# DeltaNet values: a convolution with tokens on the partitions, its shifted copies made by DMA

## The chip, the cores and the metric

The kernel runs on one core of a Trainium2 chip. The metric is the device time of one execution in microseconds (us). The engines are named as in the profile: PE (TensorE, matmuls and transposes), DVE (VectorE), ACT (ScalarE), POOL (GpSimd) and SP (SyncE, which here only issues transfers). Each engine runs its own instructions in the order in which they are written for it; engines wait for one another on semaphores.

## What is computed

Two layers of a hybrid decoder trunk for 256 tokens of width 2048. Each layer has one input projection whose columns feed a gated DeltaNet group (8 heads of 128) and an HGRN2 group; both outputs are concatenated, projected back and added, and a gated per-layer embedding is added after that. The part that matters here is the values of DeltaNet: a causal convolution over four tokens, one weight per channel and tap, then SiLU.

```python
def causal_conv(x, w):                    # x: tokens x channels, w: 4 taps x channels
    C = x.shape[-1]
    return lax.conv_general_dilated(
        x, w[:, None, :].astype(x.dtype), window_strides=(1,),
        padding=[(CONV_WIDTH - 1, 0)], dimension_numbers=("NWC", "WIO", "NWC"),
        feature_group_count=C)
...
qkv = jax.nn.silu(causal_conv(qkv.astype(f32), conv_w.astype(f32)))
q, k, v = jnp.split(qkv, 3, axis=-1)
```

So y[t] = w3·x[t] + w2·x[t−1] + w1·x[t−2] + w0·x[t−3], and v = y·sigmoid(y). The chunked delta rule then takes v scaled per token.

## The kernel before

**Weights and steps.** All large weight matrices are streamed in fp32 as 392 steps (`make_plan`, L79), most of them 128x1024 numbers, 512 KB. `load(n)` (L347) issues the transfer of a step's `raw` on SP's queue, `prep(n)` (L357) splits it: ACT rounds it to `whi` (L366), DVE subtracts to get the rest, `wlo` (L368). PE then takes three products per tile, activation-high by `whi`, activation-high by `wlo`, activation-low by `whi`, for both halves of the tokens (`products`, L380, recorded at L309): 12 matmuls for most steps. `ahead(n)` (L371) loads four steps ahead and splits two steps ahead; the pools hold three `raw` and three split pairs, so a raw buffer comes free when its `wlo` is done.

**Mixers.** The DeltaNet groups (`DN`, names `dn00` to `dn03` in layer 0 and `dn10` to `dn13` in layer 1, two heads each) and the HGRN2 groups (`HG`) are generators that are advanced once per weight step (`tick`, L331). At `yield self.wait("c")` a generator gives up PE's order for as many steps as the tables `DELAY` (L37) and `DELAY_AT` (L39) say for that point, and at `yield self.after("k")` until another part has been done. PE's instructions stay in that written order (`PEOrder`, L307); the order on DVE, ACT, POOL and SP comes from a scheduler, which weaves the mixers' work between the `wlo` and `whi` of the steps.

**The values.** `DN.dv` (L765) starts when the projection columns of `v` are complete: ACT evicts them, scaled per token, to `et` with the tokens on the partitions, 2 x 128 tokens by 256 channels (`evict`, L540, recorded at L544). A step later PE turns the four 128x128 blocks (`turned`, L547, tile `pvc`, recorded at L312), so that channels lie on the partitions and a shift by one token is a shift along the row. `conv` (L600) is then two scalings on ACT (L607) and six multiply-adds on DVE (L611); a sigmoid and a multiply (L770) give v. PE turns the four blocks back (tile `pv`), and DVE writes them, scaled by `invn` per token, to `R` (L777), which the delta rule reads. Queries and keys go through the same `conv`.

Of the kernel before, what the change touches and what calls it, by code (L numbers as in the profile page):

```python
# [8 lines left out]
F32 = mybir.dt.float32  # L9
F32R = mybir.dt.float32r  # L10
I32 = mybir.dt.int32
AF = mybir.ActivationFunctionType
ALU = mybir.AluOpType
PSUM = bass.MemoryType.PSUM

DEPTH, D, T, KT = 2, 2048, 256, 16
NG = 4
# [8 lines left out]
def chunk_cols(chunk):  # L26

    return [(START[k], 16) if k == "ba" else (START[k] + 256 * g, 256) for k, g in chunk]
# [8 lines left out]

DELAY_AT = {
# [115 lines left out]


@with_exitstack
def trunk(ctx: ExitStack, tc: tile.TileContext, head, xT, x, pT, W, par, fw, cst, msk, eye, out):
    nc = tc.nc
    pool = lambda name, bufs, **kw: ctx.enter_context(tc.tile_pool(name=name, bufs=bufs, **kw))
    cp = pool("const", 1)  # L160
# [8 lines left out]
    pm = pool("psm", 5, space=PSUM)  # L169

    V, S, G = nc.vector, nc.scalar, nc.gpsimd
# [16 lines left out]
    def xk(k, n=1):  # L188
        o = (0 if k // 4 else NNW) + T * (k % 4)
        return xt[k // 4][:, o:o + T * n]  # L190
# [54 lines left out]
    ident, ones, SL, UI = (cs[:, 128 * j:128 * j + 128] for j in range(4))  # L245
# [23 lines left out]
    def P(name, i, n=1):  # L269
        o = PAR[name][0] + i  # L270
        return pr[:, o:o + n]

    def bc(ap, n):
        return ap.unsqueeze(2).to_broadcast([ap.shape[0], ap.shape[1], n])

    def bc1(ap, n):
        return ap.unsqueeze(1).to_broadcast([ap.shape[0], n, ap.shape[1]])
# [36 lines left out]
    PE = PEOrder()  # L314
# [90 lines left out]
    def tmp(name, shape=(128, 512)):  # L405
        return tp.tile([128, 512], F32, tag="tmp", name=name)

    def sigmoid(dst, src, e=None):

        if e is None:  # L410
            S.activation(dst, src, AF.Exp, scale=-1.0)
            V.tensor_scalar(dst, dst, BIG, 1.0, ALU.min, ALU.add)
        else:
            S.activation(e, src, AF.Exp, scale=-1.0)
            V.tensor_scalar(e, e, BIG, None, ALU.min)
            V.tensor_scalar(dst, e, 1.0, None, ALU.add)
        S.activation(dst, dst, AF.Ln)
        S.activation(dst, dst, AF.Exp, scale=-1.0)
# [4 lines left out]
    def small(tag, n=4):  # L423
        return sp.tile([128, n], F32, tag=tag, name=tag)
# [36 lines left out]
    def first_squares(kp):  # L461

        sq = mp.tile([128, 512], F32, tag="R", name=f"x2{kp}", bufs=2) if not kp else tmp(f"x2{kp}")
        S.activation(sq, xk(2 * kp, 2), AF.Square)
# [46 lines left out]
    def mix(tag, n, bufs, name):  # L511
        return mp.tile([128, n], F32, tag=tag, name=name, bufs=bufs)

    def v4(ap):
        return ap.rearrange("p (a b) -> p a b", b=128)
# [24 lines left out]
    def evict(ps, c0, n, rt, name):  # L540

        et = mix("et", 1024, 2, name + "et")[:, :2 * n].rearrange("p (t n) -> p t n", t=2)
        for t in range(2):
            S.activation(et[:, t], ps[t][:, c0:c0 + n], AF.Copy, scale=rt[:, t:t + 1])  # L544
        return et

    def turned(et, c0, name):  # L547

        ps = pm.tile([128, 512], F32, tag="m", name=name)
        for i in range(4):  # L550
            hh, t = divmod(i, 2)
            PE.transpose(ps[:, 128 * i:128 * i + 128], et[:, t, c0 + 128 * hh:c0 + 128 * hh + 128], ident)
        return ps

    def rms_factor(f, ss):
        S.activation(f, ss, AF.Ln, scale=1.0 / 128, bias=epsc)
        S.activation(f, f, AF.Exp, scale=-0.5)

    class DN:
# [40 lines left out]
        def conv(self, ps, which):  # L600
# [12 lines left out]
            sigmoid(sg, ac)  # L613
            return ac, sg

        def conv_silu_kq(self, ps, which, w):
            ac, sg = self.conv(ps, which)
            for hh in range(2):
                V.tensor_tensor(self.kq[:, hh, :, w, :], v4(ac[:, 256 * hh:256 * hh + 256]),
                                v4(sg[:, 256 * hh:256 * hh + 256]), ALU.mult)  # L620
# [143 lines left out]

        def dv(self, ps, c0):  # L765
            n, kq, g = self.n, self.kq, self.g
            et = evict(ps, c0, 256, self.row.rt, n + "v")
            yield self.wait("c")
            ac, sg = self.conv(turned(et, 0, n + "pvc"), 2)
            V.tensor_tensor(ac, ac, sg, ALU.mult)  # L770
            yield self.wait("v")
            yield self.after("k")
            pv = pm.tile([128, 512], F32, tag="m", name=n + "pv")
            for i in range(4):
                PE.transpose(pv[:, 128 * i:128 * i + 128], ac[:, 128 * i:128 * i + 128], ident)
            R = v4(mix("R", 512, 2, n + "R"))
            V.tensor_tensor(R, v4(pv), bc(self.invn, 128), ALU.mult)  # L777
            yield self.after("T")
            yield self.wait("z0")
            v1 = v4(mix("v1", 512, 1, n + "v1"))  # L780

            pz = pm.tile([128, 512], F32, tag="m", name=n + "pz0")
            for hh in range(2):
                PE.matmul(pz[:, 128 * hh:128 * hh + 128], self.Tt[:, 2 * hh], R[:, 2 * hh], start=True, stop=True)
            V.tensor_tensor(v1[:, 0::2], v4(pz)[:, 0:2], bc(self.b[:, 0::2], 128), ALU.mult)
            yield self.wait("S")
            pS = pm.tile([128, 512], F32, tag="m", name=n + "pS")
            for hh in range(2):
                PE.matmul(pS[:, 128 * hh:128 * hh + 128], v4(self.ktail)[:, hh], v1[:, 2 * hh], start=True, stop=True)
            St = v4(mix("St", 256, 1, n + "St"))  # L790
            S.copy(St, v4(pS)[:, 0:2])
            yield self.wait("w")

            pw = pm.tile([128, 512], F32, tag="m", name=n + "pw")
            for hh in range(2):
                for w in range(2):
                    PE.matmul(pw[:, 256 * hh + 128 * w:256 * hh + 128 * w + 128], kq[:, hh, 1, w, :], St[:, hh],
                              start=True, stop=True)
            for hh in range(2):
                V.scalar_tensor_tensor(R[:, 2 * hh + 1], pw[:, 256 * hh:256 * hh + 128], self.neG[:, hh:hh + 1],  # L800
                                       R[:, 2 * hh + 1], ALU.mult, ALU.add)
            qs = v4(mix("qs", 256, 1, n + "qs"))
            V.tensor_tensor(qs, v4(pw)[:, 1::2], bc(self.eG, 128), ALU.mult)
            yield self.wait("z1")
            pz = pm.tile([128, 512], F32, tag="m", name=n + "pz1")
            for hh in range(2):
                PE.matmul(pz[:, 128 * hh:128 * hh + 128], self.Tt[:, 2 * hh + 1], R[:, 2 * hh + 1], start=True, stop=True)
            V.tensor_tensor(v1[:, 1::2], v4(pz)[:, 0:2], bc(self.b[:, 1::2], 128), ALU.mult)
            yield self.wait("o")
            po = pm.tile([128, 512], F32, tag="m", name=n + "po")  # L810
            for i in range(4):
                PE.matmul(po[:, 128 * i:128 * i + 128], self.QK[:, i], v1[:, i], start=True, stop=True)
            o = v4(tmp(n + "o"))
            S.copy(o[:, 0::2], v4(po)[:, 0::2])
            V.tensor_tensor(o[:, 1::2], v4(po)[:, 1::2], qs, ALU.add)
            ss = small("sso")
            for i in range(4):
                S.activation(sp.tile([128, 128], F32, tag="junk", name="junk", bufs=1), o[:, i], AF.Square,
                             scale=self.nq[:, i:i + 1], accum_out=ss[:, i:i + 1])
            f = small("fo")  # L820
            rms_factor(f, ss)
            V.tensor_tensor(f, f, self.nq, ALU.mult)
            yield self.wait("y")
            yield self.after("z")
            yield from head_norm(o, f, self.sz, P("dnw", self.l), g, self.y, n, self.wait("yp"))
# [299 lines left out]
    for l in range(DEPTH):  # L1125
# [7 lines left out]
        ps = {}  # L1133
# [16 lines left out]
        for c, k4 in order:  # L1150
# [5 lines left out]
            w = 2 if sum(n for _, n in chunk_cols(ch)) > 272 else 4  # L1156
# [26 lines left out]
        ps = {}  # L1183
# [20 lines left out]
        ps = {}  # L1204
        for c, k4 in order:
# [12 lines left out]
            if end and k4[3] == KT - 5:  # L1218

                n = state["next"]  # L1220
# [50 lines left out]
```

## Time and profile before

| what | us |
| --- | --- |
| median of 3 runs (lowest, highest) | 1284.66 (1283.68, 1284.71) |
| profiled execution | 1285.03 |
| its span, first to last instruction | 1283.3 |
| mean granted clock of PE | 0.997 |
| DMA engines, mean busy share in the tenths of the page | 4 to 8 tenths |

The profiled execution is 1.7 us longer than its span. In the page, `wlo<-raw,whi` names what an instruction writes and what it reads; `x394 | 482.9, 1227 | 257.6` are the count, the busy time in us, the mean of one in ns, and the time that the engine was idle just before such instructions. In a timeline the first number is the start, the second the duration, both in us. PE's matmuls overlap, so the distance of two starts says what one costs, not its duration.

### The profile page before, as it was taken

The page shows a single profiled execution, that of the slowest core. Times are in us where ns is not written, and L with a number is a line of the kernel's source. Part 1 is how long each engine was busy: PE and PEld are TensorE (multiplying, and loading weights), DVE is VectorE, ACT ScalarE, POOL GpSimd, SP SyncE. Part 2 cuts the span into 40 slices and gives each one's busy share as a digit, 9 for nine tenths or more (in the row PEclk, how much of TensorE's full clock was granted, in tenths as well). Part 3 has the DMA queues.
Part 4 walks back from the last instruction along what each step waited for, and adds up shares of the span by engine and source line. Part 5 has one row for each costly group of instructions (what it writes and reads, how often), then busy time and mean ns, then how long its engine had stood idle before and what let it go on. Part 6 is the DMA issues. An engine that isn't in the chain of part 4 may idle for free.

```text
span 1283.3 us, 19310 instructions
## 1 busy us (share of the span) xinstructions
PE 1262.2 (98%) x7112; PEld 1054.2 (82%) x7112; DVE 925.7 (72%) x1728; ACT 785.2 (61%) x1400; POOL 61.5 (5%) x55
## 2 busy tenths in 40 slices
PE   7999999999999999999999999999999999999996
PEld 6988888888888888888888888878888888888885
DVE  7789678787796855547568886897877958555475
ACT  7666766656665654437557667667656766544464
POOL 0100010010000000000001000100100000000010
PEclk9999999999999999999999999999999999999998
DMA  8565445445454455555555554544555545555563
GB/s 273 182 225 180 160 155 165 142 142 186 158 183 150 133 171 181 188 190 185 185 188 170 171 173 150 170 133 141 175 180 169 162 149 165 181 183 185 180 197 132
DMA packets 78751, 220.91 MB, mean 172 GB/s; under 512 B 15552, under 2 KB 25280, under 8 KB 78656
## 3 DMA queue, kind: packets, MB, share of 16 engines
q1 hardware_dynamic: 59840, 212.19, 50.9%
q10 hardware_dynamic: 18816, 7.48, 2.1%
q8 instruction: 56, 0.92, 0.3%
q14 instruction: 39, 0.32, 0.1%
HBM read 214.93 MB, written 4.72 MB: 171 GB/s over the span
## 4 chain that ended last, share of the span: by engine, by line
PE 91%; DVE 5%; ACT 1%; issue 1%; DMA 0%; SPq 0%; DVEq 0%; ACTq 0%
PE out L309 14%; PE gate L309 14%; PE in1hf L309 6%; PE in0hf L309 6%; PE in0dv L309 6%; PE in1dv L309 6%; PE in0dk L309 6%; PE in1dk L309 6%; PE in0hi L309 6%; PE in1hi L309 5%; PE up L309 2%; DVE wlo L368 1%; PE in0dz L309 1%; PE in1dz L309 1%; ACT whi L366 1%
## 5 line engine op out<-in xcount | busy, mean ns | idle before, releaser
L368 DVE TENSOR_TENSOR wlo<-raw,whi 128x1024 fp32r<-128x1024 f32 (+1 forms) x394 | 482.9, 1227 | 257.6 <-ACT whi L366 255.8
L366 ACT ACTIVATE whi<-raw 128x1024 fp32r<-128x1024 f32 (+1 forms) x394 | 413.4, 1051 | 360.7 <-PE out L309 88.3
L309 PE MATMUL in1hf<-whi,n1hi 128*128 128x512 f32 x128 | 52.5, 410 | 0.0
L309 PE MATMUL in1hi<-whi,n1hi 128*128 128x512 f32 x128 | 51.5, 402 | 0.0
L309 PE MATMUL in1dk<-whi,n1hi 128*128 128x512 f32 x128 | 51.1, 399 | 0.0
L309 PE MATMUL in1dk<-wlo,n1hi 128*128 128x512 f32 x128 | 50.1, 391 | 0.2 <-DVE wlo L368 0.2
L309 PE MATMUL gate<-whi,g0hi 128*128 128x512 f32 x128 | 50.1, 392 | 0.0
L309 PE MATMUL in1hf<-whi,n1lo 128*128 128x512 f32 x128 | 50.1, 391 | 0.0
L309 PE MATMUL in1hi<-whi,n1lo 128*128 128x512 f32 x128 | 50.0, 391 | 0.0
L309 PE MATMUL in1hf<-wlo,n1hi 128*128 128x512 f32 x128 | 50.0, 391 | 0.0
L309 PE MATMUL in1hi<-wlo,n1hi 128*128 128x512 f32 x128 | 50.0, 390 | 0.0
L309 PE MATMUL in1dk<-whi,n1lo 128*128 128x512 f32 x128 | 49.9, 390 | 0.0
L309 PE MATMUL gate<-whi,g1hi 128*128 128x512 f32 x128 | 49.9, 390 | 0.0
L309 PE MATMUL gate<-whi,g0lo 128*128 128x512 f32 x128 | 49.8, 389 | 0.0
L309 PE MATMUL gate<-wlo,g0hi 128*128 128x512 f32 x128 | 49.8, 389 | 0.0
L309 PE MATMUL gate<-whi,g1lo 128*128 128x512 f32 x128 | 49.8, 389 | 0.0
L309 PE MATMUL gate<-wlo,g1hi 128*128 128x512 f32 x128 | 49.8, 389 | 0.0
L309 PE MATMUL in1dv<-whi,n1hi 128*128 128x512 f32 (+1 forms) x128 | 48.3, 377 | 0.0
L309 PE MATMUL in1dv<-whi,n1lo 128*128 128x512 f32 (+1 forms) x128 | 46.6, 364 | 0.0
L309 PE MATMUL in1dv<-wlo,n1hi 128*128 128x512 f32 (+1 forms) x128 | 46.6, 364 | 0.0
L309 PE MATMUL in0hf<-whi,n0hi 128*128 128x512 f32 x96 | 39.2, 408 | 0.0
L309 PE MATMUL in0hi<-whi,n0hi 128*128 128x512 f32 x96 | 38.5, 401 | 0.0
(1549 smaller groups left out, 3251.2 us busy)
## 6 DMA issues: line engine op xcount, KB each, us to landing
raw<-W SPq DMA_DIRECT2D x384, 512.0 KB, 3.4
raw<-W SPq DMA_DIRECT2D x7, 544.0 KB, 4.5
h<-x SPq DMA_DIRECT2D x4, 512.0 KB, 5.4
xt<-xT SPq DMA_DIRECT2D x3, 512.0 KB, 7.0
out_dram<-h SPq DMA_DIRECT2D x6, 256.0 KB, 2.1
fw<-fw ACTq DMA_DIRECT2D x2, 512.0 KB, 5.4
pin<-pT ACTq DMA_DIRECT2D x2, 256.0 KB, 3.2
out_dram<-h ACTq DMA_DIRECT2D x2, 256.0 KB, 3.0
```

The costliest lines, as they stand in the source:

```text
L309: return tc.keep_in_program_order(nc.tensor.matmul(*a, **k))
L366: S.activation(hi[:, sl], raw[:, sl], AF.Copy)
L368: V.tensor_tensor(lo[:, sl], raw[:, sl], hi[:, sl].bitcast(F32), ALU.subtract)
```

## The change

`dv` no longer turns anything on PE. A new function `conv_tokens` leaves the tokens on the partitions: it makes three copies of `et`, shifted down by 1, 2 and 3 partitions, with transfers issued by SP. Each has a large transfer inside the columns of both token halves (L629: 127, 126 and 125 rows of 2 KB) and a small one for the rows that pass from the first half of the tokens to the second (L630); POOL zeroes the rows ahead of the first token (L628). The weights, which now vary along the row, come from a new input `cvw`, spread over 128 partitions on the host, 512 KB per group, loaded by SP (L621). DVE multiplies the unshifted tile by the last tap (L634), then each shifted tile by its tap (L636) and adds it (L637). The final scaling by `invn` and by the sigmoid goes straight to `R` in four instructions (L801). The wait "c" of the values is gone, and six distances of the mixers are other ones. `conv` stays for queries and keys. Line numbers of the changed code are those of the changed kernel.

```diff
 DELAY_AT = {
     "b1g": 5,
-    "d0D": 6, "d0k": 6, "d0p16": 4, "d0p32": 3, "d0p64": 1, "d0q": 7, "d0t64": 3, "d0v": 6,
-    "d1S": 3, "d1p64": 1, "d1q": 6, "d1ssq": 3, "d1t16": 4, "d1t32": 1, "d1yp": 2,
-    "d2D": 9, "d2k": 3, "d2t64": 4, "d2y": 4, "d2yp": 2, "d2z1": 2,
+    "d0k": 6, "d0p16": 4, "d0p32": 3, "d0p64": 1, "d0q": 7, "d0t64": 3, "d0v": 6,
+    "d1S": 2, "d1T": 8, "d1p64": 1, "d1q": 6, "d1ssq": 3, "d1t16": 4, "d1y": 4, "d1yp": 2,
+    "d2D": 9, "d2S": 2, "d2k": 3, "d2t64": 4, "d2y": 4, "d2yp": 2, "d2z1": 2,
...
+        def conv_tokens(self, ps, c0):
+            n, l, g = self.n, self.l, self.g
+            wv = mix("cvw", 1024, 1, n + "cvw")
+            nc.sync.dma_start(out=wv, in_=cvw[l * NG + g])
+            full = mix("et", 1024, 2, n + "vet")
+            et = full[:, :512]
+            for t in range(2):
+                S.activation(et[:, 256 * t:256 * t + 256], ps[t][:, c0:c0 + 256], AF.Copy, scale=self.row.rt[:, t:t + 1])
+            xs = [full[:, 512:1024], tmp(n + "vs2"), tmp(n + "vs3")]
+            for j, x in enumerate(xs, 1):
+                G.memset(x[0:j, 0:256], 0.0)
+                nc.sync.dma_start(out=x[j:128], in_=et[0:128 - j])
+                nc.sync.dma_start(out=x[0:j, 256:512], in_=et[128 - j:128, 0:256])
+            w = lambda j: bc1(wv[:, 256 * j:256 * j + 256], 2)
+            v2 = lambda ap: ap.rearrange("p (t n) -> p t n", t=2)
+            ac = tmp(n + "vac")
+            V.tensor_tensor(v2(ac), v2(et), w(3), ALU.mult)
+            for j, x in enumerate(xs, 1):
+                V.tensor_tensor(v2(x), v2(x), w(3 - j), ALU.mult)
+                V.tensor_tensor(ac, ac, x, ALU.add)
+            sg = tmp(n + "vsg")
+            sigmoid(sg, ac)
+            return ac, sg
...
         def dv(self, ps, c0):
             n, kq, g = self.n, self.kq, self.g
-            et = evict(ps, c0, 256, self.row.rt, n + "v")
-            yield self.wait("c")
-            ac, sg = self.conv(turned(et, 0, n + "pvc"), 2)
-            V.tensor_tensor(ac, ac, sg, ALU.mult)
+            ac, sg = self.conv_tokens(ps, c0)
             yield self.wait("v")
             yield self.after("k")
-            pv = pm.tile([128, 512], F32, tag="m", name=n + "pv")
-            for i in range(4):
-                PE.transpose(pv[:, 128 * i:128 * i + 128], ac[:, 128 * i:128 * i + 128], ident)
             R = v4(mix("R", 512, 2, n + "R"))
-            V.tensor_tensor(R, v4(pv), bc(self.invn, 128), ALU.mult)
+            for i in range(4):
+                hh, t = divmod(i, 2)
+                sl = slice(256 * t + 128 * hh, 256 * t + 128 * hh + 128)
+                V.scalar_tensor_tensor(R[:, i], ac[:, sl], self.invn[:, i:i + 1], sg[:, sl], ALU.mult, ALU.mult)
```

How this moves the order of instructions is shown at two places. The first is DVE around the values of group `dn11`, before (numbers behind names of `wlo` and `raw` are the step, those behind the underscore tell buffers apart):

```order
L368 TENSOR_TENSOR wlo238_7662<-raw238_7568,whi238_7661 128x1024
L412 TENSOR_SCALAR dn11sz_7651<-dn11sz_7651 128x512
L368 TENSOR_TENSOR wlo239_7712<-raw239_7627,whi239_7711 128x1024
L611 SCALAR_TENSOR_TENSOR dn11vac_7694<-dn11pvc_7689,pr_89,dn11vac_7694 128x255
L611 SCALAR_TENSOR_TENSOR dn11vac_7694<-dn11pvc_7689,pr_89,dn11vac_7694 128x254
L611 SCALAR_TENSOR_TENSOR dn11vac_7694<-dn11pvc_7689,pr_89,dn11vac_7694 128x253
L611 SCALAR_TENSOR_TENSOR dn11vac_7694<-dn11pvc_7689,pr_89,dn11vac_7694 128x255
L368 TENSOR_TENSOR wlo240_7748<-raw240_7659,whi240_7747 128x1024
```

The same place on DVE in the changed kernel, where `dn11vet` is both `et` and, in its second half, the copy shifted by one token:

```order
L634 TENSOR_TENSOR dn11vac_7681<-dn11vet_7667,dn11cvw_7665 128x512
L368 TENSOR_TENSOR wlo238_7708<-raw238_7588,whi238_7707 128x1024
L412 TENSOR_SCALAR dn11sz_7697<-dn11sz_7697 128x512
L636 TENSOR_TENSOR dn11vet_7667<-dn11vet_7667,dn11cvw_7665 128x512
L368 TENSOR_TENSOR wlo239_7738<-raw239_7647,whi239_7737 128x1024
L637 TENSOR_TENSOR dn11vac_7681<-dn11vac_7681,dn11vet_7667 128x512
L636 TENSOR_TENSOR dn11vs2_7670<-dn11vs2_7670,dn11cvw_7665 128x512
L636 TENSOR_TENSOR dn11vs3_7671<-dn11vs3_7671,dn11cvw_7665 128x512
L637 TENSOR_TENSOR dn11vac_7681<-dn11vac_7681,dn11vs2_7670 128x512
L368 TENSOR_TENSOR wlo240_7774<-raw240_7705,whi240_7773 128x1024
```

The first multiply of a shifted copy (L636) now stands ahead of the `wlo` of step 239, and four more rows ahead of that of step 240. On SP the transfers for this group stand between the weight loads of steps 240 and 241, in the changed kernel:

```order
L351 DMA raw240_7705<-W 128x1024
L630 DMA dn11vet_7667<-dn11vet_7667 1x16x16
L630 DMA dn11vs2_7670<-dn11vet_7667 2x256
L630 DMA dn11vs3_7671<-dn11vet_7667 3x256
L629 DMA dn11vet_7667<-dn11vet_7667 127x512
L629 DMA dn11vs2_7670<-dn11vet_7667 126x512
L629 DMA dn11vs3_7671<-dn11vet_7667 125x512
L351 DMA raw241_7735<-W 128x1024
```

Before, SP had only the weight loads there. The second place is DVE around the values of `dn12`, before:

```order
L368 TENSOR_TENSOR wlo271_8912<-raw271_8814,whi271_8911 128x1024
L815 TENSOR_TENSOR dn11o_8873<-dn11po_8868,dn11qs_8782 128x2x128
L701 TENSOR_TENSOR dn12pr1_8927<-dn12fx_8753 32x1
L704 TENSOR_REDUCE dn12fx_8753<-dn12pr1_8927 32x1
L701 TENSOR_TENSOR dn12pr2_8930<-dn12fx_8753 32x2x2
```

And in the changed kernel:

```order
L368 TENSOR_TENSOR wlo270_8924<-raw270_8790,whi270_8923 128x1024
L839 TENSOR_TENSOR dn11o_8865<-dn11po_8860,dn11qs_8768 128x2x128
L634 TENSOR_TENSOR dn12vac_8897<-dn12vet_8883,dn12cvw_8881 128x512
L636 TENSOR_TENSOR dn12vet_8883<-dn12vet_8883,dn12cvw_8881 128x512
L412 TENSOR_SCALAR dn12sz_8913<-dn12sz_8913 128x512
L637 TENSOR_TENSOR dn12vac_8897<-dn12vac_8897,dn12vet_8883 128x512
L636 TENSOR_TENSOR dn12vs2_8886<-dn12vs2_8886,dn12cvw_8881 128x512
L636 TENSOR_TENSOR dn12vs3_8887<-dn12vs3_8887,dn12cvw_8881 128x512
L637 TENSOR_TENSOR dn12vac_8897<-dn12vac_8897,dn12vs2_8886 128x512
L368 TENSOR_TENSOR wlo271_8942<-raw271_8842,whi271_8941 128x1024
```

The multiply of all three shifted copies and two of the additions have moved ahead of the `wlo` of step 271, which before stood ahead of all of the convolution.

More of the change, by code (lines that the diff above doesn't have):

```diff
@@ L156, in trunk @@
 @with_exitstack
-def trunk(ctx: ExitStack, tc: tile.TileContext, head, xT, x, pT, W, par, fw, cst, msk, eye, out):
+def trunk(ctx: ExitStack, tc: tile.TileContext, head, xT, x, pT, W, par, cvw, fw, cst, msk, eye, out):
     nc = tc.nc
@@ L766, in dv @@
             n, kq, g = self.n, self.kq, self.g
-            et = evict(ps, c0, 256, self.row.rt, n + "v")
-            yield self.wait("c")
-            ac, sg = self.conv(turned(et, 0, n + "pvc"), 2)
-            V.tensor_tensor(ac, ac, sg, ALU.mult)
+            ac, sg = self.conv_tokens(ps, c0)
             yield self.wait("v")
             yield self.after("k")
-            pv = pm.tile([128, 512], F32, tag="m", name=n + "pv")
+            R = v4(mix("R", 512, 2, n + "R"))
             for i in range(4):
-                PE.transpose(pv[:, 128 * i:128 * i + 128], ac[:, 128 * i:128 * i + 128], ident)
-            R = v4(mix("R", 512, 2, n + "R"))
-            V.tensor_tensor(R, v4(pv), bc(self.invn, 128), ALU.mult)
+                hh, t = divmod(i, 2)
+                sl = slice(256 * t + 128 * hh, 256 * t + 128 * hh + 128)
+                V.scalar_tensor_tensor(R[:, i], ac[:, sl], self.invn[:, i:i + 1], sg[:, sl], ALU.mult, ALU.mult)
             yield self.after("T")
@@ L1259 @@
         "par": np.ascontiguousarray(par),
+        "cvw": np.ascontiguousarray(np.broadcast_to(
+            a["dn_conv_w"][:, :, 2048:].reshape(DEPTH, 4, NG, 256).transpose(0, 2, 1, 3).reshape(DEPTH * NG, 1, 1024),
+            (DEPTH * NG, 128, 1024))),
         "fw": np.ascontiguousarray(np.broadcast_to(a["final_norm_w"], (128, D))), "cst": cst, "msk": msk,
```

## Prediction

> **What bounds the kernel now.** I read the page from its busy shares to its chain, then the waits of PE, then the costliest group of DVE.
>
> ```profile
> span 1283.3 us, 19310 instructions
> PE 1262.2 (98%) x7112; PEld 1054.2 (82%) x7112; DVE 925.7 (72%) x1728; ACT 785.2 (61%) x1400; POOL 61.5 (5%) x55
> PE 91%; DVE 5%; ACT 1%; issue 1%; DMA 0%; SPq 0%; DVEq 0%; ACTq 0%
> L368 DVE TENSOR_TENSOR wlo<-raw,whi 128x1024 fp32r<-128x1024 f32 (+1 forms) x394 | 482.9, 1227 | 257.6 <-ACT whi L366 255.8
> ```
>
> PE is busy for 98% of the span and makes 91% of the chain; the other engines only keep it fed. Its own waits, in the view of waits for PE alone, are these (total, times, longest):
>
> ```profile
> PE in0dz L309 <- ACT whi L238: 6.7, 3, 4.5
> PE dn02pv L312 <- DVE dn02vac L770: 0.7, 1, 0.7
> PE dn11pp L309 <- DVE dn11T L726: 0.7, 1, 0.7
> PE dn01pp L309 <- DVE dn01T L726: 0.7, 1, 0.7
> PE in1dk L309 <- DVE wlo L368: 0.2, 1, 0.2
> ```
>
> Apart from the start (6.7 us), PE waits for nothing worth naming: 0.2 us for `wlo`, the low half of the weights, in 392 steps. So whatever leaves PE is a gain at full price. And DVE makes every `wlo` in its own program order, 1.23 us each, with 257.6 us of idle time before them: DVE has room on average, but an instruction that stands before a `wlo` and waits for something late holds up that `wlo`, and after it PE.
>
> **What leaves PE.** Per head group 2 groups of 4 transposes, 16 groups in all. One of them in the timeline of PE, with the matmuls on both sides:
>
> ```profile
> 692.66 0.39 PE L309 MATMUL in1hf<-wlo,n1hi 128*128 128x512 f32 x1
> 692.89 0.39 PE L309 MATMUL in1hf<-whi,n1lo 128*128 128x512 f32 x1
> 693.12 0.60 PE L312 MATMUL dn10pvc<-cs,dn10vet 128*128 128x128 f32 x4
> 693.47 0.48 PE L309 MATMUL in1hf<-whi,n1hi 128*128 128x512 f32 x1
> 693.79 0.40 PE L309 MATMUL in1hf<-wlo,n1hi 128*128 128x512 f32 x1
> ```
>
> Big matmuls start 0.23 us apart. From 692.89 to 693.79 there are two of them and the group: 0.90 − 2 × 0.227 = 0.45 us. 16 × 0.45 = 7.1 us. The wait of `dn02pv`, 0.7 us, goes with it: 7.8 us gained, if nothing else becomes late.
>
> **What DVE and ACT do instead.** Rows for the durations, from the tile views and the timeline of DVE:
>
> ```profile
> L611 DVE SCALAR_TENSOR_TENSOR dn11vac<-dn11pvc,pr,dn11vac x6: 475/482/484, 777.9 to 781.3; 128x255 f32<-128x255 f32 x2, 128x254 f32<-128x254 f32 x2, 128x253 f32<-128x253 f32 x2
> 785.38 0.64 DVE L770 TENSOR_TENSOR dn11vac<-dn11vac,dn11vsg 128x512 f32<-128x512 f32 x1
> 790.57 0.69 DVE L777 TENSOR_TENSOR dn11R<-dn11pv,invn 128x512 f32<-128x512 f32 x1 [0.85 <-PE dn11pv L312]
> L800 DVE SCALAR_TENSOR_TENSOR dn11R<-dn11pw,neG,dn11R x2: 343/347/351, 882.9 to 883.1; 128x128 f32<-128x128 f32 x2
> 800.34 0.42 DVE L412 TENSOR_SCALAR hg10sz<-hg10sz 128x512 f32<-128x512 f32 x1
> 67.15 0.76 DVE L619 TENSOR_TENSOR dn00kq<-dn00qac,dn00qsg 128x256 f32<-128x256 f32 x2
> 61.82 0.47 DVE L611 SCALAR_TENSOR_TENSOR dn00qac<-dn00pqc,pr,dn00qac 128x253 f32<-128x253 f32 x1
> ```
>
> Per group DVE loses 6 × 0.48 + 0.64 + 0.69 = 4.2 us and gets 7 × 0.64 + 4 × 0.35 = 5.9 us: 1.7 us more, 8 times 13 us, beside 257.6 us of idle time; ACT loses the two scalings at L607. As throughput this is nothing. POOL's three memsets come long before their tiles are read (POOL is busy for 5%). The eight loads of `cvw` are 4 MB on a queue that moves 212 MB, and are issued a group ahead. The new distances move tiny PE groups by one step; the work that feeds them keeps its order, and the two 0.7 us waits for `pp` bound what they can give or take: I put 0, at most 1.4 either way.
>
> **The copies.** The disputed item is the copy of 127 rows of 2 KB by one row (L629), 254 KB: DVE's multiply of that tile (L636) waits for it, and stands right in front of a `wlo`. No transfer of before has a row count that 16 doesn't divide. The nearest rows:
>
> ```profile
> raw<-W SPq DMA_DIRECT2D x384, 512.0 KB, 3.4
> xt<-xT SPq DMA_DIRECT2D x3, 512.0 KB, 7.0
> dn11d<-dn11Bt ACTq DMA_DIRECT2D x1, 256.0 KB, 2.2
> q1 hardware_dynamic: 59840, 212.19, 50.9%
> ```
>
> The lower end is 2.2 us, the 256 KB of `dn11Bt`. For the upper end: 212.19 MB in 50.9% of 16 engines' 1283.3 us is 20.3 GB/s for one DMA engine; 254 KB on a single one are 12.8 us, and on 16 they are 0.8 us. So if all rows go to one engine the copy lands 2.2 − 0.8 + 12.8 = 14.2 us after its issue. 127 is prime, and the order of the changed kernel shows the same split at work: the copy of one row of 256 (L630) is issued as 16 pieces of 16, the one of 127 rows as it stands. [...]
>
> [...]
>
> What stands behind the waiting multiply, place by place: the evictions of `v` (first row: the last of the two starts at the second time, and takes 0.47 us) and the first matmul that reads the `wlo` in question.
>
> ```profile
> L544 ACT ACTIVATE dn00vet<-in0dv,s0rt x2: 473/478/482, 57.6 to 58.5; 128x256 f32<-128x256 f32 x2
> 64.71 0.39 PE L309 MATMUL in0hf<-wlo,n0hi 128*128 128x512 f32 x1
> L544 ACT ACTIVATE dn11vet<-in1dv,s1rt x2: 475/476/477, 770.1 to 771.4; 128x256 f32<-128x256 f32 x2
> 781.25 0.39 PE L309 MATMUL in1hi<-wlo,n1hi 128*128 128x512 f32 x1
> L544 ACT ACTIVATE dn12vet<-in1dv,s1rt x2: 456/462/469, 886.2 to 887.7; 128x256 f32<-128x256 f32 x2
> 897.35 0.39 PE L309 MATMUL in1hi<-wlo,n1hi 128*128 128x512 f32 x1
> L544 ACT ACTIVATE dn03vet<-in0dv,s0rt x2: 474/474/475, 332.6 to 334.0; 128x256 f32<-128x256 f32 x2
> 341.63 0.39 PE L309 MATMUL in0hf<-wlo,n0hi 128*128 128x512 f32 x1
> L544 ACT ACTIVATE dn10vet<-in1dv,s1rt x2: 455/465/475, 688.5 to 689.9; 128x256 f32<-128x256 f32 x2
> 704.21 0.39 PE L309 MATMUL in1hf<-wlo,n1hi 128*128 128x512 f32 x1
> ```
>
> - `dn00`, step 18: 59.0 + 13 + 0.64 (multiply) + 0.47 (a `qac` row) + 1.23 = 74.3, needed at 64.7: PE stalls 9.6 us.
> - `dn11`, step 239 (`dn01` has the same order): 771.9 + 13 + 0.64 + 1.23 = 786.8, needed at 781.25: 5.5 us, twice, 11 us.
> - `dn12`, step 271 (`dn02` likewise): behind the multiply stand `sz`, an addition, the second and third multiply and another addition: 888.2 + 13 + 0.64 + 0.42 + 4 × 0.64 + 1.23 = 906.0, needed at 897.35: 8.7 us; the third copy lands behind the first on its engine and may add 0.9. I take 9, twice, 18 us.
> - `dn03`, step 98 (`dn13` likewise): 334.5 + 13 + 0.64 + 1.23 = 349.4, needed at 341.6: 7.7 us; the next `wlo` has five more rows and the third copy ahead of it, which I estimate at 1.3. 9 us, twice, 18 us.
> - `dn10`, step 216: 690.4 + 13 + 0.64 + 0.76 + 4 × 0.64 + 1.23 = 708.6, needed at 704.2: 4.4 us.
>
> Together 61 us. The places lie some 80 us apart or more (58, 334 and 690, 771, 888 in the rows above), which at 257.6 idle in 1283 us leaves DVE some 16 us to catch up in, so nothing is carried over. The weight loads issued behind the copies sit on the same engine's queue, but each waits for a raw buffer that the late `wlo` itself frees, and lands some 3 to 5 us before PE, shifted by the stall, needs it: 0, with a rival for more.
>
> **Sum.** 1285.0 (this execution: its span and 1.7 us around it) − 7.8 + 61 = 1338.3; the median of the runs shown lies 0.4 below the profiled execution: 1338.
>
> **The rivals.**
> A (forecast): one engine carries the 127 rows. The sum moves by 8 us for each us of the landing: at 11 us 1322, at 15 us 1354. Likeliest range 1316 to 1360.
> B, the other side: the rows spread over the engines as every transfer of before does, and land after 2.2 us. DVE's order then has room at all eight places (in `dn12` 888.2 + 2.2 + 0.64 + 0.42 + 2.56 + 1.23 = 895.3, needed at 897.35), and only PE's relief is left: 1284.7 − 7.8, and some 1 us back at `dn00`, where DVE is fullest: 1278. For it: the largest transfers of before land within 7.0 us (`xt`, twice the size, at the crowded start). Against it: 127 can't be dealt out evenly, and the single row was cut on purpose. The mechanism decides at a landing of about 6 us: there `dn00` (2.6), `dn02` and `dn12` (2 each), `dn03` and `dn13` (0.7 each) eat the 7.8.
> C: one engine, and the loads queued behind the copies are late as well. Then it is as if the landing took 3 us more: 24 us on top, 1362. For it: SP issues both. Against it: the buffers, above.
> D: one engine that is about twice as fast, so that landing and gain cancel: 1285. Against it: the row of q1.
>
> **Chances.** A 0.79, C 0.06, B 0.13, D 0.02. Differences under 0.2% (2.6 us) can't be told from no change. Faster 0.13 (B), same 0.02 (D), slower 0.85 (A and C). The predicted time is A's. For the range I reach from a landing of 9 us (1306, lower still if a place hides more than I think: 1302) to C's 1366; B is left out whole, with what A and C have outside, not quite 2 in 10.
>
> **What would show it.** Right: the copies `vet<-vet` of 254 KB land about 13 us after their issue, those of 126 rows a little after them on the queue; PE's view of waits gets eight entries, `in..hf` and `in..hi` of layers 0 and 1 on DVE `wlo`, of 4 to 10 us each and about 60 us together; the idle time before DVE's L636 is about as large as the copies take; PE's busy time falls by some 7 us. Wrong: if the copies land in 2 to 3 us, the forecast falls whole and B holds; if they are late but PE waits for `raw` and `whi` instead of `wlo`, it is C; if they are late and PE doesn't wait, I have misread the order of DVE.

## The result

The changed kernel takes 1370.03 us (median of 4 runs, 1369.76 to 1372.78) against 1284.68 us: 1.0667 times as long, with a 95% interval of 1.0654 to 1.0680. The sign and the mechanism were as forecast, the size was not: 85 us were lost where 53 were forecast, and the time lies 4 us above the range.

The profile after, in the order of the prediction's views. First the page:

```profile
span 1368.0 us, 19330 instructions
PE 1272.7 (93%) x7048; PEld 1057.5 (77%) x7048; DVE 937.2 (69%) x1752; ACT 779.5 (57%) x1384; POOL 84.7 (6%) x79
PEclk9989999989989999999999999999898999999998
PE 82%; DMA 8%; DVE 6%; ACT 1%; issue 1%; SPq 1%; ACTq 0%; DVEq 0%
```

PE's share falls from 98% to 93%, and DMA, which had no part in the chain, has 8% of it. But PE is also busy for 10.5 us more than before with 64 instructions fewer, and the row of the granted clock has gaps that it did not have. Then the waits of PE (total, times, longest):

```profile
PE in0hf L309 <- DVE wlo L368: 21.3, 2, 12.0
PE in0hi L309 <- DVE wlo L368: 19.1, 2, 12.0
PE in1hi L309 <- DVE wlo L368: 18.7, 2, 11.6
PE in1hf L309 <- DVE wlo L368: 10.5, 3, 9.3
PE in0dz L309 <- ACT whi L238: 5.7, 3, 4.6
PE dn10pg L309 <- DVE dn10kq L645: 5.1, 1, 5.1
PE in0dk L309 <- DVE wlo L368: 1.3, 1, 1.3
PE in1dk L309 <- DVE wlo L368: 0.8, 1, 0.8
PE dn10px L309 <- ACT dn10P L761: 0.8, 1, 0.8
```

They add up to 83.3 us, where the five rows of before make 9.0: 74.3 us more. With the 10.5 us of busy time this is the whole difference of the spans, 1368.0 − 1283.3 = 84.7 us. And this is what `wlo` waited behind, in the waits of DVE:

```profile
DVE dn03vet L636 <- DMA dn03vet<-dn03vet: 12.7, 1, 12.7
DVE dn13vet L636 <- DMA dn13vet<-dn13vet: 12.7, 1, 12.7
DVE dn01vet L636 <- DMA dn01vet<-dn01vet: 11.5, 1, 11.5
DVE dn11vet L636 <- DMA dn11vet<-dn11vet: 11.4, 1, 11.4
DVE dn02vet L636 <- DMA dn02vet<-dn02vet: 10.8, 1, 10.8
DVE dn00vet L636 <- DMA dn00vet<-dn00vet: 10.5, 1, 10.5
DVE dn12vet L636 <- DMA dn12vet<-dn12vet: 10.5, 1, 10.5
DVE dn10vet L636 <- DMA dn10vet<-dn10vet: 10.3, 1, 10.3
```

Eight places, one for each group, each a wait of the first multiply for the copy of 127 rows. The rows of the tile `dn11vet` give the landing: SP issues that copy at 826.8, 0.6 us after the eviction, and the multiply starts at 840.4, 13.6 us later (at the eight places 13.6 to 15.0 us):

```profile
L629 SPq DMA_DIRECT2D dn11vet<-dn11vet x1: 631/631/631, 826.8 to 826.8; - x1
L636 DVE TENSOR_TENSOR dn11vet<-dn11vet,dn11cvw x1: 691/691/691, 840.4 to 840.4; 128x512 f32<-128x512 f32 x1
```

The one engine can be seen directly. Up to 831.0 SP is still issuing the next copy, so that only the 127 rows are under way, and the view of stretches of time (each row: the stretch, its length, busy time of PE, weight loads, DVE, ACT and POOL, then clock, DMA share and GB/s) gives

```profile
830.00:831.50 1.50, 1.50 (x9) 1.22 (x8) 0.00 (x0) 0.63 (x1) 0.77 (x1) 1.00 0.07 26
```

One of 16 engines is a share of 0.06, and at 26 GB/s the 254 KB take 10.0 us.

The busy time is in the timeline of PE, at the end of the stall of `dn00`:

```profile
75.84 0.79 PE L309 MATMUL in0hf<-wlo,n0hi 128*128 128x512 f32 x1 [12.04 <-DVE wlo L368]
76.43 0.63 PE L309 MATMUL in0hf<-whi,n0lo 128*128 128x512 f32 x1
76.86 0.63 PE L309 MATMUL in0hf<-whi,n0hi 128*128 128x512 f32 x1
...
81.47 0.39 PE L309 MATMUL in0hf<-wlo,n0hi 128*128 128x512 f32 x1
81.70 0.39 PE L309 MATMUL in0hf<-whi,n0lo 128*128 128x512 f32 x1
```

Behind the stall matmuls start 0.43 us apart, and only some 5 us later 0.23 us apart again. The stretches of time with the granted clock show why (the stall begins at 75.84 − 12.04 = 63.8):

```profile
63.80:67.00 3.20, 0.00 (x1) 0.00 (x0) 0.00 (x0) 0.87 (x1) 0.00 (x0) 1.00 0.32 103
67.40:75.80 8.40, 0.00 (x0) 0.00 (x0) 2.23 (x4) 0.63 (x1) 0.00 (x0) 0.50 0.14 45
75.80:80.60 4.80, 4.76 (x11) 3.69 (x12) 4.80 (x9) 1.26 (x2) 1.93 (x1) 0.50 0.66 199
81.20:83.00 1.80, 1.80 (x10) 1.49 (x9) 1.47 (x2) 1.47 (x8) 1.80 (x1) 1.00 0.61 228
```

PE idles, its clock is halved, and it works on at half speed before full speed is granted again: here the clock falls 3.2 to 3.6 us after PE went idle and is back at 1.00 some 5 us after work resumed. In steps of 0.2 us, the same view gives 2.0 to 4.8 us for the fall at the eight stalls, and 3.1 to 5.4 us for the return. A shorter stall can be enough, as one of 1.9 us below shows. The prediction's sum had no term for any of this.

### The profile page after: what moved, and what is told of

Same layout as the page of the kernel before. It is cut to its first block, busy times and chain, and to the rows that moved or that the text cites. A ratio compares the mean times of both kernels' runs of the same rounds, so it can differ in the third digit from the quotient of the medians.

```text
span 1368.0 us, 19330 instructions
## 1 busy us (share of the span) xinstructions
PE 1272.7 (93%) x7048; PEld 1057.5 (77%) x7048; DVE 937.2 (69%) x1752; ACT 779.5 (57%) x1384; POOL 84.7 (6%) x79
## 2 busy tenths in 40 slices
DMA packets 83422, 231.33 MB, mean 169 GB/s; under 512 B 16136, under 2 KB 25904, under 8 KB 83328
## 4 chain that ended last, share of the span: by engine, by line
PE 82%; DMA 8%; DVE 6%; ACT 1%; issue 1%; SPq 1%; ACTq 0%; DVEq 0%
PE out L309 13%; PE gate L309 13%; PE in0hi L309 6%; PE in1hi L309 6%; PE in0dv L309 6%; PE in1dv L309 6%; PE in0dk L309 5%; PE in1dk L309 5%; PE in0hf L309 5%; PE in1hf L309 4%; DVE wlo L368 2%; PE up L309 2%; DMA dn10vet<-dn10vet 1%; DMA dn00vet<-dn00vet 1%; PE in0dz L309 1%
## 5 line engine op out<-in xcount | busy, mean ns | idle before, releaser
L366 ACT ACTIVATE whi<-raw 128x1024 fp32r<-128x1024 f32 (+1 forms) x394 | 413.5, 1051 | 404.2 <-PE out L309 88.3
L309 PE MATMUL in1hi<-wlo,n1hi 128*128 128x512 f32 x128 | 52.0, 406 | 18.7 <-DVE wlo L368 18.7
L309 PE MATMUL in1hf<-wlo,n1hi 128*128 128x512 f32 x128 | 51.1, 399 | 10.5 <-DVE wlo L368 10.5
L309 PE MATMUL in0hf<-wlo,n0hi 128*128 128x512 f32 x96 | 39.5, 411 | 21.4 <-DVE wlo L368 21.3
L309 PE MATMUL in0hi<-wlo,n0hi 128*128 128x512 f32 x96 | 39.4, 411 | 19.1 <-DVE wlo L368 19.1
```

Of the source, the lines that this page charges most:

```text
L309: return tc.keep_in_program_order(nc.tensor.matmul(*a, **k))
L366: S.activation(hi[:, sl], raw[:, sl], AF.Copy)
```

## The experiments

The theory to be tested: the copy of 127 rows goes through one DMA engine, because no number up to 16 but 1 divides 127, and DVE, waiting for it in program order, starves PE. The rivals: the copies are slow for another reason (their place on SP's queue, or SBUF to SBUF over one partition as such); the new order of DVE costs by itself; the slow matmuls have a cause other than the stall.

**Cut by rows.** All three copies are cut, so that by the theory 16, 15, 14 and 13 engines share the parts:

```diff
-                nc.sync.dma_start(out=x[j:128], in_=et[0:128 - j])
+                nc.sync.dma_start(out=x[j:112 + j], in_=et[0:112])
+                nc.sync.dma_start(out=x[112 + j:128], in_=et[112:128 - j])
```

> The three shifted copies are cut by rows: 112 rows in one transfer, the remaining 15, 14 or 13 in a second; nothing else changes. Theory (the 127 rows go through one DMA engine because 127 has no divisor up to 16; 112 has 16): the copies land 2 to 4 us after their issue, DVE waits less than 1 us at each L636, PE waits for wlo less than 5 us in all instead of 72, and the time is 1274 to 1282 us, under the kernel before by what PE no longer does (7.8 us). Rival 1 (a copy from SBUF to SBUF over one partition is slow however it is cut): over 1330. Rival 2 (the new order on DVE costs by itself, without the late copy): 1290 to 1310.

Measured: 1284.09 us against 1285.31, a ratio of 0.9993 (0.9984 to 1.0002). The whole loss is gone with this one change. The copy of `dn11` is now issued in two parts at 776.5 and 777.1, and the multiply starts at 780.3 without a wait. DVE's waits for the copies shrink to two, 1.0 us at `dn12` and 0.5 us at `dn13`. But the time is that of the kernel before, not 7.8 us less, and above the 1274 to 1282 that were expected. The longest waits of PE in this kernel say where the gain is:

```profile
PE in0dz L309 <- ACT whi L238: 7.3, 2, 4.5
PE in0dk L309 <- DVE wlo L368: 4.3, 3, 3.7
PE in0hf L309 <- DVE wlo L368: 1.4, 1, 1.4
```

and the timeline of PE at the longest of them:

```profile
105.78 0.80 PE L309 MATMUL in0dk<-wlo,n0hi 128*128 128x512 f32 x1 [3.71 <-DVE wlo L368]
106.38 0.63 PE L309 MATMUL in0dk<-whi,n0lo 128*128 128x512 f32 x1
```

Two stalls for `wlo` in the first 110 us, of 1.4 and 3.7 us, and the longer one brings half-speed matmuls as well. Both lie around `dn00`.

**Two engines.** Only the copy of 127 rows is cut, into 122 = 2 x 61 rows and 5:

```diff
-                nc.sync.dma_start(out=x[j:128], in_=et[0:128 - j])
+                m = 122 if j == 1 else 128 - j
+                nc.sync.dma_start(out=x[j:m + j], in_=et[0:m])
+                if j == 1:
+                    nc.sync.dma_start(out=x[m + j:128], in_=et[m:128 - j])
```

> Only the copy of 127 rows is cut, into 122 and 5 rows. 122 is 2 x 61, so by the theory two engines carry 61 rows each: at the 0.1 us per row of the changed kernel it lands some 7 to 8 us after the eviction instead of 14, PE stalls at dn00, dn02, dn12, dn03 and dn13 by 2 to 5 us each and nearly not at the others: 1290 to 1312. Rival (the count of rows doesn't decide): as the changed kernel, 1365 to 1375, or, if any cut helps, as with 112 rows, under 1283.

Measured: 1336.82 us (one execution), above the expected 1312 and well under the 1365 of the rival. DVE waits 5.2 to 7.2 us at the eight places instead of 10.3 to 12.7:

```profile
DVE dn13vet L639 <- DMA dn13vet<-dn13vet: 7.2, 1, 7.2
DVE dn11vet L639 <- DMA dn11vet<-dn11vet: 5.2, 1, 5.2
PE dn00px L309 <- ACT dn00P L764: 6.2, 1, 6.2
PE dn10px L309 <- ACT dn10P L764: 5.3, 1, 5.3
```

For `dn11`, `dn12` and `dn03` the multiply starts 9.1, 8.8 and 9.1 us after the issue, against 13.6, 13.9 and 13.6 with 127 rows: by the theory's count 66 rows fewer on an engine save 4.7 us, 0.07 us a row, and some 4.7 us do not depend on the rows. (Over all eight places it is 8.8 to 11.1 us against 13.6 to 15.0.) The direction is the theory's; the size was missed since the fixed part is larger than 1.4 us, and since PE now waits 11.5 us for two evictions `P` of the mixers, which ACT could only do after a weight tile that landed late (in the timeline of ACT it waits 5.1 us for `raw` ahead of the second of them).

**The queue.** The three uncut copies issued by ACT (`nc.scalar` for `nc.sync` in L629):

> The copies of 127, 126 and 125 rows are issued by ACT instead of SP, uncut. Theory (the DMA engine is the limit, not the queue): the 127 rows still land 12 to 15 us after the eviction, and the time stays at 1355 to 1385. Rival (they are late because they stand on SP's queue behind 512 KB weight loads): they land within 5 us, and the time falls under 1300.

Measured: 1398.79 us (one execution), above what was expected. The 127 rows land as late as on SP: DVE waits 10.4 to 13.2 us for them, and in `dn11` the multiply starts 13.3 us after the issue. So SP's queue is not what makes them slow. The extra 29 us go with ACT: PE waits for it in rows that the changed kernel does not have, 11.9 and 11.8 us for `Tt` of `dn02` and `dn12` and 9.2 us for `whi`. The tile views show long issues on ACT's queue: in `dn12` that of the copy of 127 rows lasts 0.66 us, but the next one, begun at 975.7, lasts 4.17 us, and the third begins at 980.0. That the waits for `Tt` come from such stretches is argued, not shown.

**Only the first copy cut**, into 112 and 15 rows; 126 and 125 rows stay whole:

```diff
+                m = 112 if j == 1 else 128 - j
```

with the rest as in the kernel with two engines.

> The changed kernel with only the copy of 127 rows cut (112 and 15), those of 126 and 125 rows left whole. Theory (126 = 14 x 9 and 125 = 5 x 25, so 14 and 5 engines carry them with 9 and 25 rows each, at 0.1 us a row): they land within 2 and 4 us, 1284 to 1292, near e1_split. Rival (every row count that 16 doesn't divide is bad): over 1320.

Measured: 1293.36 us against 1285.21, a ratio of 1.0062 (1.0032 to 1.0093), just outside what was expected and far under the rival's 1320. An indivisible number of rows is not bad as such, only what it leaves on one engine: with 25 rows on each of 5 engines the third copy of `dn03` is issued at 340.7 and its multiply starts at 348.3, and DVE waits up to 3.9 us there. In the middle of that wait five of the 16 engines are busy, a share of 0.33:

```profile
345.00:347.00 2.00, 2.00 (x11) 1.54 (x9) 0.00 (x0) 0.00 (x0) 0.00 (x0) 1.00 0.33 109
```

**PE kept busy.** Ahead of the steps that stall, PE gets matmuls that nobody reads:

```diff
+        if n in FILL:      # {18: 48, 43: 28, 75: 48, 98: 37, 239: 28, 271: 48, 294: 37}
+            kp, kj = divmod(s["kts"][0], 2)
+            dummy = pm.tile([128, 512], F32, tag="m", name=f"fill{n}")
+            for _ in range(FILL[n]):
+                PE.matmul(dummy[:, :s["n"]], act[kp][0][:, T * kj:T * kj + 128], ready[n][0][0], start=True, stop=True)
```

> At the steps where PE stalls in seven of the eight places (all but dn10) PE gets matmuls whose result nobody reads, 28 to 48 of 128x512, about as many as fill the stall, so that it is busy while it waits. Theory (the slow matmuls behind each stall come from a clock that is lowered because PE idled): the matmuls behind the places start 0.23 us apart from the first on, the granted clock rises from 0.967 to over 0.99, and the time falls by 12 to 18 us, to 1352 to 1358. Rival (they are slow for another reason, such as operands that have just been written, or the filler takes what it saves): within 4 us of 1370.

Measured: 1411.13 us, so the expectation for the time was wrong, and the granted clock rose only to 0.978. PE is busy with the 274 fillers and has new waits elsewhere, such as 7.4 us for `whi` twice and 6.6 and 6.5 us for `St`; that the scheduler counts the fillers as PE time and moves other rows is argued, not shown. The total says nothing about the clock, therefore. The place of `dn00` does, since its stall ends at the same time in both kernels (75.84 before the filler, 75.83 with it):

```profile
75.83 0.50 PE L312 MATMUL in0hf<-wlo,n0hi 128*128 128x512 f32 x1 [0.33 <-DVE wlo L371]
76.16 0.40 PE L312 MATMUL in0hf<-whi,n0lo 128*128 128x512 f32 x1
76.40 0.39 PE L312 MATMUL in0hf<-whi,n0hi 128*128 128x512 f32 x1
...
81.66 1.89 PE L312 MATMUL dn00pg<-dn00kq 128*128 128x256 f32 x8
```

With PE busy until 0.33 us earlier, the same matmuls run at full speed at once, and `dn00pg` starts at 81.66 instead of 84.00: the half-speed stretch costs 2.3 us here, and it comes from the idling, not from the operands.

**A copy that nobody reads.** The kernel before, with one copy of 127 rows per group:

```diff
             et = evict(ps, c0, 256, self.row.rt, n + "v")
+            ghost = v4(mix("ghost", 512, 1, n + "ghost")).rearrange("p (t h) n -> p t (h n)", t=2)
+            nc.sync.dma_start(out=ghost[1:128], in_=et[0:127])
```

> The kernel before, with one copy of 127 rows per group added on SP, from et to a tile that nobody reads; all else as before. It asks what the slow copy costs when no engine waits for it. Theory A (its one engine also carries a sixteenth of every weight load queued behind it, so those land late): ACT waits for raw at some of the eight places, 1 to 3 us of stall each, 1288 to 1302. Theory B (only the waiting multiply on DVE costs): 1283 to 1287.

Measured: 1321.77 us against 1285.05, a ratio of 1.0290 (1.0275 to 1.0306): 36.7 us, more than either theory said, with no instruction that waits for the copy. Of the 34.5 us by which the span grows, 19.9 are waits of PE and 14.2 its busy time, at a granted clock of 0.989 instead of 0.997. The waits of ACT for `raw`, in this kernel:

```profile
ACT whi L366 <- DMA raw<-W: 61.5, 13, 8.3
```

In the kernel before, that row reads 9.6 us in 6 waits. Theory A reads it so: a weight load has a sixteenth of its rows on the engine that carries the copy, and lands when that part has landed. Two kernels take this apart. The first issues the same copy from ACT (`nc.scalar`):

> As e7_ghost (the kernel before, plus one unread copy of 127 rows per group), but issued by ACT, so that no weight load stands behind it on its queue. e7_ghost cost 37 us, and ACT waited 61.5 us for raw there. Theory A (order within one queue: a load waits for the copy ahead of it on that engine): without the queue the cost goes almost whole, 1285 to 1292, ACT waits for raw under 20 us. Theory B (the one DMA engine is shared by the queues, so a load's sixteenth on it is slowed anyhow): a good part stays, 1296 to 1320.

Measured: 1298.05 us against 1285.21, 1.0096 (1.0066 to 1.0126). Some 24 of the 37 us go, so most of the cost comes with SP's queue, on which the weight loads stand. But 13 us stay, which puts the time in theory B's range and not in theory A's, with ACT waiting 31.3 us for `raw` in 24 short waits of at most 2.3 us. How much of the rest is the shared engine and how much the time that ACT spends on issuing (0.66 us for such a copy in the kernel with the copies on ACT's queue) is not settled. The second cuts the unread copy into 112 and 15 rows:

> e7_ghost with the unread copy cut into 112 and 15 rows. Theory (it is the rows on one engine that cost, not the bytes or the transfer): within 3 us of the kernel before, 1283 to 1288. Rival (any added transfer between the weight loads costs): over 1292.

Measured: 1285.26 us against 1285.21, 1.0002 (0.9991 to 1.0013). The same bytes, spread, cost nothing. That a load's part waits on the engine for the copy ahead of it on SP's queue is theory A's reading; the three kernels agree with it as far as the 24 us go that the other queue saves.

**The distances.** The kernel before with the new `DELAY_AT`, nothing else:

> The kernel before with the six new distances and nothing else. Theory (the distances are worth at most the two 0.7 us waits): 1283 to 1287, within 0.15% of the kernel before. Rival (the distances carry part of what the version with cut copies gains or loses): off by more than 2.5 us.

Measured: 1285.94 us against 1285.05, 1.0007 (0.9998 to 1.0016): worth nothing to the old convolution. Then the cut copies with the old `DELAY_AT`:

> Cut copies (112 rows and the rest) as in e1_split, but with the distances of the kernel before. In e1_split PE waited 5.5 us for wlo at steps 18 and 29 (3.7 and 1.4 us, then matmuls at half the clock), and that is where the gain of PE's missing transposes went. Theory (the wait "D" of dn00, 4 steps instead of 6, brings more DVE rows ahead of the wlo of step 18 and so starts both): the waits shrink to under 2 us, 1278 to 1281. Rival (the cause is the new convolution in dn00 itself, whose rows DVE has no room for at the start): both waits stay, 1283 to 1286.

Measured: 1298.03 us against 1285.05, 1.0094 (1.0079 to 1.0109), the opposite of what was expected: 13 us worse than before, where the same copies with the new distances are level. The waits of PE:

```profile
PE dn11yp L312 <- DVE dn11yt L522: 3.5, 2, 3.3
PE dn01yp L312 <- DVE dn01yt L522: 3.5, 2, 3.3
PE dn00pg L309 <- DVE dn00kq L646: 1.7, 1, 1.7
PE in0dk L309 <- DVE wlo L368: 1.6, 1, 1.6
PE dn12pS L309 <- DVE dn12v L810: 1.5, 1, 1.5
```

`yp` of group 1 and `pS` of group 2 come too early for the new load of DVE; these are two of the places (`d1y`, `d2S`) to which the new table gives one step more. Around `dn00`, though, this kernel loses less than the cut copies with the new table. So one distance alone goes back, `d0D` to 6:

```diff
-    "d0k": 6, "d0p16": 4,
+    "d0D": 6, "d0k": 6, "d0p16": 4,
```

> e1_split with one of the six distances as before: wait "D" of dn00 6 steps again, not 4. In e6_split_old_dist, with all six as before, PE lost about 4 us around dn00 where e1_split loses 8, but 8 more at dn01, dn02, dn11 and dn12. Theory (the early "D" is what crowds DVE at dn00, and the other five distances are what the new convolution needs): PE's waits at steps 18 and 29 shrink, no new ones come, 1278 to 1281. Rival (the crowding comes from the new convolution in dn00 itself, as e8_first_old suggests): 1283 to 1286, as e1_split.

Measured: 1280.87 us against 1284.71, 0.9966 (0.9954 to 0.9978), in the range of the theory: part of the loss at `dn00` was this distance. The waits bear the theory out only in part. In the profiled execution, with 1284.0 us the slowest of the six, those around `dn00` shrink from 5.7 to 3.6 us (1.9 at `in0dk`, 1.7 at `dn00pg`), and one of 1.9 us at `in1dk` is new. The two of 1.9 us differ in what follows: behind that of `in0dk`, at 103.2, eight matmuls start 0.43 us apart, the spacing that goes with a granted clock of 0.50 in the changed kernel; behind that of `in1dk` none does, and the mean granted clock, 0.996 against 0.997 before, has room for one such stretch (3.7 us at half speed are 0.0014 of the span), not for two.

**The first group as before.** The cut copies, with the old convolution in `dn00` alone:

```diff
+            if self.l == 0 and g == 0:
+                et = evict(ps, c0, 256, self.row.rt, n + "v")
+                yield self.wait("c")
+                ac, sg = self.conv(turned(et, 0, n + "pvc"), 2)
...
+            else:
+                ac, sg = self.conv_tokens(ps, c0)
```

> e1_split with the old convolution (transposes, taps per partition) for the values of dn00 alone, seven groups with cut copies, new distances. Theory (in e1_split the gain is lost to DVE's crowded stretch at dn00): the waits at steps 18 and 29 go, seven eighths of the 7.8 us remain, 1277 to 1280. Rival (it is lost to the loads of cvw or to small waits spread over all groups): 1282 to 1286.

Measured: 1276.04 us against 1285.05, 0.9928 (0.9916 to 0.9941), 1 us below what the theory had. Its page and all of PE's waits:

```profile
PE 1255.2 (99%) x7056; PEld 1048.3 (82%) x7056; DVE 939.1 (74%) x1749; ACT 780.2 (61%) x1386; POOL 80.1 (6%) x76
PE in0dz L309 <- ACT whi L238: 6.1, 3, 4.5
PE in1dk L309 <- DVE wlo L368: 0.4, 1, 0.4
```

With seven groups changed and the first left alone, PE hardly waits any more after the start, and 9 us are gained: 14 groups of transposes at 0.45 us are 6.3, the three 0.7 us waits of before (`dn02pv` and the two `pp`) 2.1, and a little at the start. This is the fastest of all kernels here, and beats both that were compared.

## Why the prediction was wrong

- **What bounds the kernel, and where DVE stands.** Right. All of PE's new waits but one short row are on DVE, and DVE's eight waits are those of the eight multiplies at L636 that the prediction listed.
- **One engine for 127 rows.** Right, though it was my estimate: no run shows the 13 us that the sums use, and what the runs showed in their place is 13.6 to 15.0 us from the issue to the use. On the number of engines: 127 rows on one engine are used 13.6 to 15.0 us after their issue, 61 rows on each of two, by the theory's count, after 8.8 to 11.1, and with 112 and 15 rows at most 1.0 us of the wait is left; the queue is not the cause. The DMA shares of 0.07 with 127 rows and 0.33 with 125 are those of one and five of 16 engines. The pages count packets, too. The eight unread copies of 127 rows bring 1024 of them (60864 against 59840 on the queue), 128 a copy, and one of these is under 512 B (15560 against 15552). The changed kernel has 16136 under 512 B, 16376 with the first copy cut and 16696 with all three: 30 and 70 more per group, as if there were one for each engine, 16 + 15 in place of 1, then 16 + 14 in place of 14 and 16 + 13 in place of 5. That each engine adds one is my reading. The working behind the 14.2 us, from which the 13 come, was less good than its result, and that is luck: a row costs 0.07 to 0.08 us (two engines against one; 26 GB/s) and not 0.1, and the fixed part is 4 to 5 us and not 1.4; the two errors nearly cancel.
- **The stalls, 61 us: too small, 74.7 us.** By place, forecast and measured: `dn00` 9.6 and 12.0, `dn01` and `dn02` together 14.5 and 19.1, `dn11` and `dn12` 14.5 and 18.7, `dn03` 9 and 9.3, `dn10` and `dn13` 13.4 and 15.6. I let the copy land 13 us after the eviction, below the 14.2 that my sum had as its upper end; it is used 13.9 to 15.0 us after it, 14.4 on the mean. At `dn01`, `dn03`, `dn11` and `dn13` 0.6 to 0.7 us of this are small transfers that SP issues first; at the other four the issue follows the eviction at once. Taken over eight places the 1.4 us are 11 of the 14 that are missing, but the places do not follow it one by one: at `dn03` and `dn13` the stall is only 0.3 us longer than forecast, at `dn02` and `dn12` 3.0 and 2.6. There DVE also waits 0.8 us for one of the other two copies, for which the sum had 0.9, an estimate too. What the rest is there stays open.
- **The clock: the step that was left out.** The sum had no term for what PE does after a stall. Each of the eight stalls brings a stretch at a granted clock of 0.50, which costs 2.3 us in the comparison with the filler. Over the kernel: PE's busy time rose by 10.5 us where the transposes take 7.1 away, 17.6 us in all. The page of before hides it, with a mean clock of 0.997, but the timeline of PE before has it once, behind the wait of 4.5 us at the start:

```profile
12.33 0.43 PE L309 MATMUL in0dz<-whi,n0alo 128*128 128x272 f32 x1
12.55 0.43 PE L309 MATMUL in0dz<-whi,n0ahi 128*128 128x272 f32 x1
...
12.95 0.29 PE L309 MATMUL in0dz<-whi,n0alo 128*128 128x272 f32 x1
13.07 0.29 PE L309 MATMUL in0dz<-whi,n0ahi 128*128 128x272 f32 x1
```

The same matmuls start 0.22 us apart up to 12.55 and 0.12 us apart from 12.95 on. That this is the clock is read from the spacing alone, as the view gives a clock of 1.00 for that stretch. With the stalls as forecast and 2 us behind each, the sum would have been 1354, inside the range; with the stalls as measured too, it is the 1370 that came.
- **"The weight loads behind the copies: 0".** Wrong as reasoning, though it does not show in the time of this kernel. The copy that nobody reads costs 36.7 us though no instruction waits for it. In the changed kernel ACT waits 44.8 us for `raw`, but no row of PE's waits names the `whi` (L366) that ACT makes of it; that the two delays run side by side is how I read this. Rival C had the mechanism and added the delays, which was wrong too.
- **The gain, 7.8 us.** Right for PE, but not free: with fast copies it is eaten in `dn00`, where DVE has no room in the crowded start, and comes out (9 us) when that group keeps the old convolution. Rival B's 1278 would thus have been 1284 for this order of DVE.
- **The distances, 0, at most 1.4 either way.** True for the old convolution (1.0007), wrong for the new one: with cut copies the old table costs 1.0094 and the new one 0.9993. They could not be priced by the waits of before, because they answer to waits that only the new order makes.

## What to carry to other kernels

Ask of each transfer that an in-order engine waits for how its rows divide over the DMA engines: a copy shifted by one partition has 127 rows, and cutting the three copies at 112 rows was worth 86 us here, 77 of them with the first copy alone. A copy that nobody waits for is not free either, when the weights stand behind it on the same queue: eight cost 36.7 us here. And price a stall of PE with what follows it: behind each of the eight stalls here, 5.1 to 12.0 us long, the first matmuls ran at a granted clock of 0.50, and PE's busy time grew by 17.6 us beside the stalls.

## What was not expected of the hardware

An unread copy of 254 KB in 127 rows cost 4.6 us on the mean (36.7 us for eight), against nothing when cut into 112 and 15 rows. PE's half clock set in after a stall as short as 1.9 us in one place, though not after another of that length, and lasted for 8 to 11 matmuls at 0.43 us in the places told of here. And 125 rows, at a DMA share of 0.33, that of five engines, took 7.6 us from issue to use, far more than a fifth of the 13.6 to 15.0 us of the 127 rows: most of such a copy's time, by this comparison, is the part that doesn't depend on its rows.
